# A Hymba block: FF2's forms staged by POOL four ahead, FF1's first products before the last transposes, the residual by adding transfers

## The chip, the cores and the metric

The kernel runs on one core of a Trainium2 chip. The metric is the device time of one execution in microseconds (us). TensorE (PE) multiplies, VectorE (DVE) and ScalarE (ACT) do arithmetic on tiles, GpSimd (POOL) and SyncE (SP) here mostly issue transfers (DMAs), each from its own queue and in its own order. TensorE's clock has two levels, 1.2 and 2.4 GHz; the profile gives the granted clock as a share of the full one.

## What is computed

One layer on x of 512 rows (SEQ) and 2048 columns (D), in float32:

```
u = rmsnorm(x, g1);  z = u @ w_in           # conv B, C, h, gla q, k, v, gate, decay
y = concat(conv_group(z), gla_group(z))
x = x + y @ w_out
h = rmsnorm(x, g2)
x = x + square(relu(h @ w_ff1)) @ w_ff2     # w_ff1: 2048 x 8192
out = rmsnorm(x, gf)
```

## The kernel before

**Products.** A float32 operand is split into a rounded part hi (ACT, a cast) and the rest lo (DVE, a subtraction); a product is hi x hi + hi x lo + lo x hi on PE. Both layers of the feed-forward part use a scheme of seven products in place of eight: an operand's four quarters are combined into seven *forms*, each product multiplies one form of the activations by one form of the weights, and sums of the results give the four quarters of the output. A product of a form is 24 matmuls of 128 x 128 by 128 x 256.

**The stages.** In-projection, gates, gated linear attention (`gla`), convolution; the out-projection in five chunks of columns (`out_chunk`, `token_major`), whose `put` adds the residual into xr (L602), squares it on ACT (L604) and stores it to x_keep. `h_pair(p)` transposes two 128-column tiles of xr on PE (htr, L563), scales them on DVE (h, L564), forms differences (L568 to L572) and splits the seven forms into Sh (ACT, L589) and Sl (DVE, L590). The last pair, 7, stands behind the whole out-projection.

FF1 runs over 32 groups g of two column tiles; a group loads four quarters of weights (SP, L494), forms sums (w_f, DVE, L509), splits them (hi_f L501, lo_f L502), and does seven products in the order 1, 5, 7, 3, 6, 2, 4 (`product`, L643, PE L653) into banks f1a to f1e. DVE and ACT combine, relu and square (L684 to L695). The seven forms of the result go to a_keep in HBM (POOL).

FF2 runs over four blocks (blk) of the contraction, in each over four column groups n and two halves grp: seven products each (`product2`, PE L747), the last half of block 3 with half the length. `form(blk, grp, f)` loads a form back from a_keep into st (SP, L729), casts ah (ACT, L735) and subtracts al (DVE, L736). Of the seven forms of a half every second is loaded into one of two stage buffers, the others into tiles of `act` that FF1's or an earlier block's forms held. `form` is called behind the product whose slots it takes over: the other half's forms during n = 0, the next block's during the last half of n = 3. `evict` (L768) sums the results into four tiles c, which POOL adds to c_keep in HBM (L774, L776); in block 3 tiles s are loaded from c_keep (L839), c is added into them by a transfer (L780), and `residual` (L756, DVE) adds s times r2 to x3, which was loaded from x_keep (L835). A last stage (PE e, L75 to L77) multiplies what is left of the contraction, adds, normalizes and writes.

**What sets the order.** The program is written in the order of the products; a scheduler then sets each engine's own order, and pools set which tile must be free. The weights' hi and lo have three buffers each, the raw quarters four, the sums w_f two. Lines that the change touches: L372 (GLA's states, pool of two), L603 (squares into a bank of tag "one"), L620 (`h_pair(7)`), L630 (PSUM pools change from `front` to `fb`), L644 to L656 (`product`), L718 to L738 (`form`), L751 to L758 (`residual`).

Of the kernel before, what the change touches and what calls it, by code (L numbers as in the profile page):

```python
# [8 lines left out]
F32 = mybir.dt.float32  # L9
# [5 lines left out]
P = 128  # L15
# [24 lines left out]
def hymba_kernel(  # L40
# [150 lines left out]
    with tc.tile_pool(name="mix", bufs=1) as mix:  # L191
# [167 lines left out]
        def gla(h):  # L359
# [4 lines left out]
            for c in range(NCHUNK):  # L364
                i = c // 2
                r = slice(c % 2 * CHUNK, (c % 2 + 1) * CHUNK)
                kv = bank(f"kv_{c}{h}", "one")
                T.matmul(
                    kv[:, :DV], kd[r, i, h * DK : (h + 1) * DK], vv[h // 2][r, i, cv],
                    start=True, stop=True,  # L370
                )
                st = mix.tile([P, DV], F32, name=f"st_{c}{h}", tag="st", bufs=2)  # L372
                if c == 0:
                    V.tensor_copy(st, kv[:, :DV])
                else:
# [221 lines left out]
    with tc.tile_pool(name="n2", bufs=1) as n2:  # L597

        def out_chunk(n, wsrc, w0, nunit, ncol, ktu, hook, ready=()):
            def put(i, b):  # L600
                xc = xs[n][i]
                V.tensor_tensor(out=xc, in0=b[:, :ncol], in1=xc, op=ALU.add)  # L602
                sq = bank(f"sq2_{n}{i}", "one")  # L603
                S.activation(sq[:, :ncol], xc, AF.Square, accum_out=ss2[:, i, n : n + 1])  # L604
                nc.gpsimd.dma_start(x_keep[i][:, chunks[n]], xc)

            token_major(yt, wsrc, w0, nunit, ncol, ktu, f"op{n}", put, hook, None, ready)
# [10 lines left out]
        first_forms = block_forms(w_ff1, 0, 1024, "f1_0")  # L618
        ready = {f: first_forms(f) for f in (1, 5, 7)}
        h_pair(7, n2)  # L620
        a2 = n2.tile([P, NT], F32, name="a2", tag="a2")
# [7 lines left out]
    late.close()  # L629
    front.close()  # L630
    fb = ctx.enter_context(tc.tile_pool(name="fb", bufs=1, space=PSUM, reuse_waits="tile"))

# [4 lines left out]


    with tc.tile_pool(name="f1", bufs=1, reuse_waits="tile") as f1:
        for g in range(NPAIR):  # L640
            forms = block_forms(w_ff1, 4 * g, 1024, f"f1_{g}") if g else first_forms

            def product(f, dst, start, pairs=range(8)):  # L643
                if g or f not in ready:  # L644
                    ready[f] = forms(f)
                hi, lo = ready[f]
                if 7 in pairs:
                    del ready[f]
                for p in pairs:
                    c = slice(p * P, (p + 1) * P)  # L650
                    sh, sl = hforms[p][f]
                    for m, (l, r) in enumerate(((hi, sh), (hi, sl), (lo, sh))):
                        T.matmul(  # L653
                            dst[:, :HALF], l[:, c], r, start=start and p == m == 0,
                            stop=p == 7 and m == 2, skip_group_check=True,
                        )  # L656
# [4 lines left out]
            ba, bc, bd, bb, be = (fbank(f"f1{k}_{g}") for k in "acdbe")  # L661
# [46 lines left out]


    PLACE = {1: 0, 2: 1, 4: 2, 7: 3, 5: 4, 6: 5, 3: 6}  # L710
    ORDERS = ((1, 3, 2, 5, 7, 6, 4), (1, 6, 5, 3, 7, 2, 4))
    first = [(hf, f"h{n}") for n in range(14)]
    second = [(act, f"s{k + 8 * m}") for e in range(2) for k in range(e, 8, 2) for m in range(2)]

    def in_slot(slot, name, dt=F32R):
        return slot[0].tile([P, 4, HALF], dt, name=name, tag=slot[1])

    with tc.tile_pool(name="ff", bufs=1, reuse_waits="tile") as ff:  # L718

        def form(blk, grp, f):  # L720

            n = ORDERS[grp].index(f)
            m = 2 if (blk, grp) == (3, 1) else 4
            name = f"st_{blk}{grp}{f}"
            if n % 2 and (blk, grp) != (3, 1):
                raw = in_slot(second[14 + n // 2 % 2], name, F32)
            else:
                raw = stage.tile([P, 4, HALF], F32, name=name, tag="st", bufs=2)
            nc.sync.dma_start(raw[:, :m, :], a_keep[2 * blk + grp][PLACE[f]][:, :m, :])  # L729
            if m == 2:  # L730
                t = in_slot(second[n], f"a{blk}{grp}{f}")
                hi, lo = t[:, 0:2, :], t[:, 2:4, :]
            else:
                hi, lo = (in_slot((first, second)[grp][2 * n + e], f"a{'hl'[e]}{blk}{grp}{f}") for e in range(2))
            S.copy(hi[:, :m, :], raw[:, :m, :])  # L735
            V.tensor_tensor(out=lo[:, :m, :], in0=raw[:, :m, :], in1=hi[:, :m, :].bitcast(F32), op=ALU.subtract)  # L736
            aforms[blk, grp, f] = hi, lo

# [62 lines left out]

        aforms = {}
        x3t = None
        for f in ORDERS[0]:
            form(0, 0, f)
        for blk in range(4):
            for n in range(4):
                dst = {f: fbank(f"f2_{blk}{n}{f}") for f in ORDERS[1]}
                had = {}
                for grp in range(2):  # L810
# [6 lines left out]
                    for f in ORDERS[grp]:  # L817
# [50 lines left out]
        for g in range(2):  # L868
            raw = stage.tile([P, 4, HALF], F32, name=f"st_e{g}", tag="st", bufs=2)
            nc.sync.dma_start(raw, a_last[g])  # L870
# [3 lines left out]
        for n in order[1:]:  # L874
            last_weights(n)
        gft = [stage.tile([P, 4, HALF], F32, name=f"gft{c}", tag="st", bufs=2) for c in range(2)]
        for c in range(2):
# [115 lines left out]
```

## Time and profile before

| | us |
|---|---|
| median of 3 runs (2109.1 to 2111.61) | 2111.08 |
| the profiled execution | 2109.2 |
| its span in the trace | 2107.5 |
| PE busy in it | 2070.4 |
| DVE busy | 1489.1 |
| ACT busy | 885.2 |
| POOL busy | 130.3 |

PE is busy for 98% of the span, so a step matters by what it does to PE's stops and to PE's clock. Three kinds of views are used: lists of waits (for whom an engine stood idle, how long in total, how often, the longest), windows (the busy time of each engine in a stretch, the mean granted clock, the busy share of the 16 DMA engines), and timelines (single instructions). In a timeline a row with x2 or x3 holds that many instructions, and the bracket gives the idle time ahead of it and what ended it.

### The profile page before, as it was taken

Reading aid. Unit: us, or ns where it says so; the run is one execution under the profiler, and the core shown is the slowest. Engines: PE = TensorE matmul, PEld = TensorE weight load, DVE = VectorE, ACT = ScalarE, POOL = GpSimd, SP = SyncE. Lnnn points to the kernel's source line nnn. Section 1 sums busy time; section 2 is a strip of 40 time slices with the busy share of each in tenths; the row PEclk is TensorE's granted clock in tenths of the full one; section 3 lists DMA queues with packets and bytes.
Section 4 is the critical chain, followed back from the end, with each engine's and each line's share of the span. In section 5 each row is a group of like instructions: output and inputs, shape, how many; then the busy total and the mean of one; then the engine's idle time right before and its main releaser. Section 6 shows DMA issues by size and latency. Waiting matters only on the chain. (4 is left out here: it accounts for less than half of the span.)

```text
span 2107.5 us, 34328 instructions
## 1 busy us (share of the span) xinstructions
PE 2070.4 (98%) x14408; PEld 1920.4 (91%) x14408; DVE 1489.1 (71%) x1740; ACT 885.2 (42%) x1106; POOL 130.3 (6%) x197
## 2 busy tenths in 40 slices
PE   8999999999999999999999999998999999999998
PEld 7988878778788899999999999998999999999996
DVE  5232226656664458888888888888789789888987
ACT  6242213212233334555555455555344345344343
POOL 0000000000010000000000000000000100103210
PEclk9999999999999999999999999999999999999999
DMA  7323222222253333544544544547456657667762
GB/s 296 90 80 100 90 86 85 80 80 89 72 159 122 121 117 114 180 153 145 164 153 137 165 152 143 163 156 255 144 166 216 148 158 219 166 158 237 182 187 101
DMA packets 90427, 307.11 MB, mean 146 GB/s; under 512 B 10773, under 2 KB 10821, under 8 KB 89760
## 3 DMA queue, kind: packets, MB, share of 16 engines
q1 hardware_dynamic: 69120, 242.64, 36.9%
q0 software_dynamic: 21152, 62.28, 10.5%
q8 instruction: 112, 1.84, 0.4%
q14 instruction: 43, 0.35, 0.1%
HBM read 252.19 MB, written 49.55 MB: 143 GB/s over the span
## 5 line engine op out<-in xcount | busy, mean ns | idle before, releaser
L747 PE MATMUL f<-hi_f,ah 128*128 128x256 f32 x1568 | 442.2, 282 | 10.9 <-ACT hi_f L501 5.6
L747 PE MATMUL f<-lo_f,ah 128*128 128x256 f32 x1568 | 444.0, 283 | 4.5 <-DVE lo_f L502 4.5
L747 PE MATMUL f<-hi_f,al 128*128 128x256 f32 x1568 | 441.1, 282 | 0.0
L502 DVE TENSOR_TENSOR lo_f<-w_f,hi_f 128x1024 fp32r<-128x1024 f32 (+1 forms) x256 | 304.2, 1191 | 144.3 <-ACT hi_f L501 142.8
L501 ACT CAST hi_f<-w_f 128x1024 fp32r<-128x1024 f32 (+1 forms) x256 | 261.8, 1024 | 337.0 <-PE f L747 113.9
L747 PEld LDWEIGHTS f<-hi_f,ah 128*128 128x128 f32 x1568 | 297.0, 189 | 12.9 <-ACT hi_f L501 7.2
L747 PEld LDWEIGHTS f<-lo_f,ah 128*128 128x128 f32 x1568 | 296.5, 189 | 6.9 <-DVE lo_f L502 6.5
L747 PEld LDWEIGHTS f<-hi_f,al 128*128 128x128 f32 x1568 | 297.1, 190 | 0.0
L501 ACT CAST hi_f<-raw_f 128x1024 fp32r<-128x1024 f32 (+1 forms) x192 | 196.6, 1025 | 197.5 <-PE f L747 84.3
L502 DVE TENSOR_TENSOR lo_f<-raw_f,hi_f 128x1024 fp32r<-128x1024 f32 (+1 forms) x192 | 227.9, 1187 | 25.9 <-ACT hi_f L501 25.9
L509 DVE TENSOR_TENSOR w_f<-raw_f,raw_f 128x1024 f32<-128x1024 f32 (+1 forms) x128 | 152.4, 1190 | 12.9 <-DMA raw_f<-in_w_ff 9.7
L509 DVE TENSOR_TENSOR w_f<-w_f,raw_f 128x1024 f32<-128x1024 f32 (+1 forms) x128 | 152.4, 1190 | 3.3
L653 PE MATMUL f1c<-Sh,hi_f 128*128 128x256 f32 x512 | 144.2, 282 | 0.9 <-ACT q L676 0.9
L653 PE MATMUL f1a<-Sh,hi_f 128*128 128x256 f32 x512 | 144.9, 283 | 0.0
L653 PE MATMUL f1a<-Sh,lo_f 128*128 128x256 f32 x512 | 144.9, 283 | 0.0
L653 PE MATMUL f1a<-Sl,hi_f 128*128 128x256 f32 x512 | 144.7, 283 | 0.0
L653 PE MATMUL f1c<-Sh,lo_f 128*128 128x256 f32 x512 | 144.2, 282 | 0.2 <-DVE lo_f L502 0.2
L653 PE MATMUL f1c<-Sl,hi_f 128*128 128x256 f32 x512 | 144.0, 281 | 0.0
L75 PE MATMUL tm_op<-hi_op,yh 128*128 128x512 f32 (+1 forms) x304 | 106.2, 349 | 0.0
L76 PE MATMUL tm_op<-lo_op,yh 128*128 128x512 f32 (+1 forms) x304 | 105.3, 346 | 0.0
L77 PE MATMUL tm_op<-hi_op,yl 128*128 128x512 f32 (+1 forms) x304 | 105.0, 345 | 0.0
L653 PEld LDWEIGHTS f1c<-Sh,hi_f 128*128 128x128 f32 x512 | 96.8, 189 | 1.1 <-ACT q L676 1.1
(360 smaller groups left out, 4857.8 us busy)
## 6 DMA issues: line engine op xcount, KB each, us to landing
raw_f<-in_w_ff SPq DMA_DIRECT2D x240, 512.0 KB, 3.6
a_keep<-y POOLq DMA_DIRECT2D x30, 896.0 KB, 5.1
st<-a_keep SPq DMA_DIRECT2D x49, 512.0 KB, 4.5
c_keep<-c POOLq DMA_DIRECT2D x48, 256.0 KB, 5.3
raw_op<-in_w_out SPq DMA_DIRECT2D x22, 512.0 KB, 3.6
raw_og<-in_w_feat SPq DMA_DIRECT2D x16, 512.0 KB, 3.6
raw_cc<-in_w_feat SPq DMA_DIRECT2D x16, 512.0 KB, 3.6
raw_ch<-in_w_feat SPq DMA_DIRECT2D x16, 512.0 KB, 3.7
```

Source lines behind the costliest of these rows:

```text
L75: T.matmul(dst, l[0], r[0], start=start, stop=False)
L76: T.matmul(dst, l[0], r[1], start=False, stop=False)
L77: T.matmul(dst, l[1], r[0], start=False, stop=stop)
L501: S.copy(hi[:, :n], src)
L502: V.tensor_tensor(out=lo[:, :n], in0=src, in1=hi[:, :n].bitcast(F32), op=ALU.subtract)
L509: V.tensor_tensor(out=w, in0=in0, in1=in1, op=ALU.add)
L653: T.matmul(dst[:, :HALF], l[:, c], r, start=start and p == m == 0, stop=p == 7 and m == 2, skip_group_check=True,)
L747: T.matmul(d, l[:, k, t], r[:, c], start=grp == k == i == e == 0, stop=grp == 1 and k == m - 1 and e == 2, skip_group_check=True,)
```

## The change

1. GLA's states get four buffers.
2. The squares of `put` go into the bank that held the sum, not into one of tag "one".
3. The products 1, 5 and 7 of FF1's group 0 over pairs 0 to 6 (63 matmuls) are written ahead of `h_pair(7)`. Group 0 uses banks of the `front` pools; these close at group 1.
4. Forms of FF2 are loaded by POOL into one of four stage buffers (`stage_form`); the load of form q + 4 is issued behind the split of form q (`split_form`), and an agenda says behind which product each form is split. The old `form` goes.
5. For n < 3 `residual` scales s by r2 on ACT and lets a transfer of POOL add it to x3.

```diff
-                st = mix.tile([P, DV], F32, name=f"st_{c}{h}", tag="st", bufs=2)
+                st = mix.tile([P, DV], F32, name=f"st_{c}{h}", tag="st", bufs=4)
...
-                sq = bank(f"sq2_{n}{i}", "one")
-                S.activation(sq[:, :ncol], xc, AF.Square, accum_out=ss2[:, i, n : n + 1])
+                S.activation(b[:, :ncol], xc, AF.Square, accum_out=ss2[:, i, n : n + 1])
...
         ready = {f: first_forms(f) for f in (1, 5, 7)}
+        def multiply(f, dst, start, pairs=range(8)):
+            hi, lo = ready[f]
...
+        first_banks = {1: bank("f1a_0", "one"), 5: bank("f1c_0", "one"), 7: bank("f1d_0")}
+        for f in (1, 5, 7):
+            multiply(f, first_banks[f], True, range(7))
         h_pair(7, n2)
...
-    front.close()
-    fb = ctx.enter_context(tc.tile_pool(name="fb", bufs=1, space=PSUM, reuse_waits="tile"))
...
+    sequence = [(blk, grp, f) for blk in range(4) for grp in range(2) for f in ORDERS[grp]]
+
+    def stage_form(q):
+
+        blk, grp, f = sequence[q]
+        m = 2 if (blk, grp) == (3, 1) else 4
+        raw = stage.tile([P, 4, HALF], F32, name=f"st_{blk}{grp}{f}", tag="st", bufs=4)
+        nc.gpsimd.dma_start(raw[:, :m, :], a_keep[2 * blk + grp][PLACE[f]][:, :m, :])
+        staged[q] = raw, m
+
+    def split_form(q):
+        blk, grp, f = sequence[q]
+        raw, m = staged.pop(q)
...
+        S.copy(hi[:, :m, :], raw[:, :m, :])
+        V.tensor_tensor(out=lo[:, :m, :], in0=raw[:, :m, :], in1=hi[:, :m, :].bitcast(F32), op=ALU.subtract)
+        aforms[blk, grp, f] = hi, lo
+        if q + 4 < len(sequence):
+            stage_form(q + 4)
...
+    agenda = {-10: [lambda: [stage_form(q) for q in range(4)]]}
+    for q in range(len(sequence)):
+        blk, k = divmod(q, 14)
+        if k >= 7:
+            at = 56 * blk + int((0 if blk else 2) + 1.4 * (k - 7))
+        else:
+            at = 56 * blk - 14 + int(5 + 1.35 * k) if blk else k - 4
+        agenda.setdefault(at, []).append(lambda q=q: split_form(q))
...
+            if g == 1:
+                front.close()
+                fb = ctx.enter_context(tc.tile_pool(name="fb", bufs=1, space=PSUM, reuse_waits="tile"))
...
             if g == 0:
-                for f, b in ((1, ba), (5, bc), (7, bd)):
-                    product(f, b, True, range(7))
...
+                if n < 3:
+                    S.activation(c[:, i, :], c[:, i, :], AF.Copy, scale=r2[:, k : k + 1])
+                    nc.gpsimd.dma_start(xc, c[:, i, :], accum_op=ALU.add)
+                    continue
...
-                        if (n, grp) == (0, 0):
-                            form(blk, 1, f)
-                        if (n, grp) == (3, 1) and blk < 3:
-                            form(blk + 1, 0, ORDERS[0][ORDERS[1].index(f)])
+                        keep_agenda(7 * (8 * blk + 2 * n + grp) + ORDERS[grp].index(f))
```

The agenda and the scheduler move instructions at three places. The first is PE's order at the end of the out-projection (tm_op43 is the last of its banks, xr_40 to xr_43 are the last sums, htr the transposes, f1a, f1c, f1d the banks of products 1, 5, 7; Sh1 and Sh70 are high parts of pairs 0 to 3 and of pair 7). Before:

```order
L77 MATMUL tm_op43_5330<-hi_op4_3_5566,yl_7_4078 128x256
L563 MATMUL htr_14_5660<-ident_72,xr_40_4160 128x128
...
L563 MATMUL htr_15_5666<-ident_72,xr_40_4160 128x128
...
L563 MATMUL htr_14_5660<-ident_72,xr_43_4163 128x128
L563 MATMUL htr_15_5666<-ident_72,xr_43_4163 128x128
L653 MATMUL f1a_0_5707<-Sh1_4547,hi_f1_01_5643 128x256
L653 MATMUL f1a_0_5707<-Sl1_4548,hi_f1_01_5643 128x256
L653 MATMUL f1a_0_5707<-Sh1_4547,lo_f1_01_5644 128x256
```

and now:

```order
L77 MATMUL tm_op43_5314<-hi_op4_3_5550,yl_7_4078 128x256
L628 MATMUL f1a_0_5639<-Sh1_4543,hi_f1_01_5623 128x256
L628 MATMUL f1a_0_5639<-Sl1_4544,hi_f1_01_5623 128x256
L628 MATMUL f1a_0_5639<-Sh1_4543,lo_f1_01_5624 128x256
...
L628 MATMUL f1d_0_5641<-Sh60_5541,hi_f1_07_5635 128x256
L628 MATMUL f1d_0_5641<-Sl60_5542,hi_f1_07_5635 128x256
L628 MATMUL f1d_0_5641<-Sh60_5541,lo_f1_07_5636 128x256
L563 MATMUL htr_14_5706<-ident_72,xr_40_4160 128x128
...
L563 MATMUL htr_14_5706<-ident_72,xr_43_4163 128x128
...
L563 MATMUL htr_15_5712<-ident_72,xr_43_4163 128x128
L628 MATMUL f1c_0_5640<-Sh70_5721,hi_f1_05_5629 128x256
L628 MATMUL f1a_0_5639<-Sh70_5721,hi_f1_01_5623 128x256
L628 MATMUL f1d_0_5641<-Sh70_5721,hi_f1_07_5635 128x256
L628 MATMUL f1c_0_5640<-Sl70_5722,hi_f1_05_5629 128x256
```

The eight transposes stood ahead of all 72 matmuls of the first three products; now 63 of these stand ahead of them, and behind them the nine that need pair 7.

The second is ACT's order from the last group of FF1 into FF2 (ah_blk,grp,form are casts of forms; hi_f1_31x are weights of FF1's last group, hi_f2_000x those of FF2's first products). Before:

```order
L735 CAST ah002_13215<-st_002_13213 128x1024
...
L735 CAST ah007_13227<-st_007_13225 128x1024
L501 CAST hi_f2_0001_13258<-raw_f2_0000_13250 128x1024
...
L735 CAST ah004_13239<-st_004_13237 128x1024
L735 CAST ah011_13288<-st_011_13286 128x1024
...
L735 CAST ah003_13209<-st_003_13207 128x1024
L735 CAST ah005_13221<-st_005_13219 128x1024
L735 CAST ah015_13392<-st_015_13390 128x1024
L735 CAST ah017_13428<-st_017_13426 128x1024
L501 CAST hi_f2_0007_13398<-w_f2_0007_13396 128x1024
```

and now:

```order
L683 CAST ah001_13087<-st_001_12876 128x1024
...
L683 CAST ah003_13122<-st_003_12878 128x1024
...
L683 CAST ah002_13162<-st_002_12880 128x1024
...
L683 CAST ah005_13197<-st_005_12882 128x1024
L501 CAST hi_f1_314_13169<-w_f1_315_12997 128x1024
L683 CAST ah007_13256<-st_007_13091 128x1024
L501 CAST hi_f2_0001_13228<-raw_f2_0000_13220 128x1024
L683 CAST ah006_13290<-st_006_13126 128x1024
```

The form 003, which the second product of FF2 needs, was cast behind 002, 007, 004 and 011; now it is the second, ahead of three weights of FF1's last group.

The third is ACT's order in block 3 where n goes from 0 to 1 (s_0q are the sums of n = 0, hi_f2_310x the weights of n = 1). Before:

```order
L501 CAST hi_f2_3103_19339<-raw_f2_3102_19305 128x1024
L501 CAST hi_f2_3102_19369<-raw_f2_3103_19307 128x1024
L501 CAST hi_f2_3105_19401<-w_f2_3105_19399 128x1024
L501 CAST hi_f2_3107_19433<-w_f2_3107_19431 128x1024
L501 CAST hi_f2_3106_19462<-w_f2_3105_19399 128x1024
```

and now:

```order
L501 CAST hi_f2_3103_19321<-raw_f2_3102_19285 128x1024
L792 ACTIVATE s_00_19113<-s_00_19113,r2_4185 128x256 x2
L501 CAST hi_f2_3102_19353<-raw_f2_3103_19287 128x1024
L792 ACTIVATE s_02_19117<-s_02_19117,r2_4185 128x256 x2
L792 ACTIVATE s_01_19115<-s_01_19115,r2_4185 128x256 x2
L501 CAST hi_f2_3105_19387<-w_f2_3105_19385 128x1024
L792 ACTIVATE s_03_19119<-s_03_19119,r2_4185 128x256 x2
L501 CAST hi_f2_3107_19421<-w_f2_3107_19419 128x1024
L501 CAST hi_f2_3106_19450<-w_f2_3105_19385 128x1024
```

The pairs that scale s stand between the casts of weights; those of s_03 are ahead of the cast for product 7. On POOL, the issues of the same stretch were four and are now:

```order
L819 DMA s_02_19117<-c2_30_19232 128x512
L819 DMA s_01_19115<-c1_30_19251 128x512
L793 DMA x3_00_19097<-s_00_19113 128x256
L793 DMA x3_10_19099<-s_00_19113 128x256
L793 DMA x3_20_19101<-s_02_19117 128x256
L819 DMA s_03_19119<-c3_30_19271 128x512
L793 DMA x3_30_19103<-s_02_19117 128x256
L793 DMA x3_01_19098<-s_01_19115 128x256
L793 DMA x3_11_19100<-s_01_19115 128x256
```

The transfer that adds c3 to s_03 stands behind three that add s to x3, and so behind ACT's pairs for s_00 and s_02.

## Rows read from the trace of the kernel before

**Rows 1.** The page, busy us (share) x instructions of each engine.
```profile
PE 2070.4 (98%) x14408; PEld 1920.4 (91%) x14408; DVE 1489.1 (71%) x1740; ACT 885.2 (42%) x1106; POOL 130.3 (6%) x197
```

**Rows 2.** Waits of PE, whole span: us in total, times, longest.
```profile
PE f L747 <- ACT hi_f L501: 5.6, 8, 0.9
PE f L747 <- DVE lo_f L502: 5.6, 11, 0.9
```

**Rows 3.** Windows: us, busy PE, PEld, DVE, ACT, POOL, clock, DMA share, GB/s.
```profile
780.00:800.00 20.00, 16.51 (x125) 16.00 (x124) 17.57 (x33) 8.26 (x17) 2.17 (x4) 0.91 0.08 27
1430.00:1450.00 20.00, 15.38 (x118) 15.18 (x117) 16.22 (x16) 14.17 (x16) 0.55 (x1) 0.91 0.90 314
1600.00:1620.00 20.00, 17.73 (x139) 16.58 (x139) 18.81 (x18) 7.43 (x8) 0.54 (x1) 1.00 0.77 250
1760.00:1780.00 20.00, 17.92 (x148) 17.28 (x146) 17.90 (x17) 8.61 (x10) 1.08 (x2) 1.00 0.92 254
1930.00:1940.00 10.00, 8.24 (x54) 7.83 (x54) 6.56 (x8) 4.71 (x6) 6.03 (x12) 0.83 0.97 306
```

**Rows 4.** Timeline of PE, 784 to 802: start us, duration us, instruction.
```profile
785.09 0.28 PE L77 MATMUL tm_op<-hi_op,yl 128*128 128x256 f32 x1
...
789.81 0.44 PE L563 MATMUL htr<-ident,xr 128*128 128x128 f32 x2 [3.15 <-DVE xr L602]
...
794.10 0.28 PE L653 MATMUL f1c<-Sh,hi_f 128*128 128x256 f32 x1
794.22 0.29 PE L653 MATMUL f1c<-Sl,hi_f 128*128 128x256 f32 x1
...
801.18 0.39 PE L653 MATMUL f1c<-Sh,hi_f 128*128 128x256 f32 x1 [0.85 <-ACT q L676]
```

**Rows 5.** Timeline of DVE, 779 to 803.
```profile
787.33 2.09 DVE L590 TENSOR_TENSOR Sl<-h,Sh 128x768 fp32r<-128x768 f32 x2
...
790.80 1.40 DVE L564 SCALAR_TENSOR_TENSOR h<-htr,g2t,r1b 128x512 f32<-128x512 f32 x2
...
792.20 1.22 DVE L509 TENSOR_TENSOR w_f<-raw_f,raw_f 128x1024 f32<-128x1024 f32 x1
...
796.34 1.22 DVE L590 TENSOR_TENSOR Sl<-h,Sh 128x1024 fp32r<-128x1024 f32 x1
```

**Rows 6.** Timeline of ACT, 779 to 803.
```profile
789.85 0.39 ACT L604 ACTIVATE sq<-xr 128x256 f32<-128x256 f32 x1 [0.95 <-DVE xr L602]
...
799.54 1.05 ACT L501 CAST hi_f<-raw_f 128x1024 fp32r<-128x1024 f32 x1 [3.23 <-PE f1c L653]
```

**Rows 7.** Timelines of PE and DVE at the change from FF1 to FF2.
```profile
1439.00 0.58 PE L747 MATMUL f<-hi_f,ah 128*128 128x256 f32 x1 [4.62 <-ACT ah L735]
...
1426.46 0.42 DVE L684 TENSOR_TENSOR u<-f1b,q 128x256 f32<-128x256 f32 x1
...
1453.83 1.22 DVE L502 TENSOR_TENSOR lo_f<-w_f,hi_f 128x1024 fp32r<-128x1024 f32 x1
```

**Rows 8.** Waits of ACT in 1885 to 1945 (block 2 to 3).
```profile
ACT a L735 <- DMA st<-a_keep: 15.0, 7, 4.1
```

**Rows 9.** DMA: issues (KB, median us to landing); landings of tile s, of c_keep.
```profile
st<-a_keep SPq DMA_DIRECT2D x49, 512.0 KB, 4.5
...
gft<-in_gf POOLq DMA_DIRECT2D x2, 512.0 KB, 4.1
...
DMA to landing us min/median/max: 2.9/3.9/5.7
...
DMA to landing us min/median/max: 2.3/4.9/8.5
```

**Rows 10.** Timelines of POOL and PE in block 3, n = 0 to 1.
```profile
1988.24 1.76 POOL L780 DMA_DIRECT2D s<-c  x2 [0.30 <-DVE c L768]
...
1988.64 0.38 PE L747 MATMUL f<-hi_f,ah 128*128 128x256 f32 x1 [0.90 <-ACT hi_f L501]
...
1993.35 0.34 PE L747 MATMUL f<-lo_f,ah 128*128 128x256 f32 x1
```

More of the change, by code (lines that the diff above doesn't have):

```diff
@@ L619, in hymba_kernel @@
         ready = {f: first_forms(f) for f in (1, 5, 7)}
+        def multiply(f, dst, start, pairs=range(8)):
+            hi, lo = ready[f]
+            if 7 in pairs:
+                del ready[f]
+            for p in pairs:
+                c = slice(p * P, (p + 1) * P)
+                sh, sl = hforms[p][f]
+                for m, (l, r) in enumerate(((hi, sh), (hi, sl), (lo, sh))):
+                    T.matmul(
+                        dst[:, :HALF], l[:, c], r, start=start and p == m == 0,
+                        stop=p == 7 and m == 2, skip_group_check=True,
+                    )
+        first_banks = {1: bank("f1a_0", "one"), 5: bank("f1c_0", "one"), 7: bank("f1d_0")}
+        for f in (1, 5, 7):
+            multiply(f, first_banks[f], True, range(7))
         h_pair(7, n2)
@@ L636, in hymba_kernel, with in_slot @@
     stage = ctx.enter_context(tc.tile_pool(name="stage", bufs=1, reuse_waits="tile"))
+    PLACE = {1: 0, 2: 1, 4: 2, 7: 3, 5: 4, 6: 5, 3: 6}
+    ORDERS = ((1, 3, 2, 5, 7, 6, 4), (1, 6, 5, 3, 7, 2, 4))
+    first = [(hf, f"h{n}") for n in range(14)]
+    second = [(act, f"s{k + 8 * m}") for e in range(2) for k in range(e, 8, 2) for m in range(2)]
+    def in_slot(slot, name, dt=F32R):
+        return slot[0].tile([P, 4, HALF], dt, name=name, tag=slot[1])
+    aforms = {}
+    staged = {}
+    sequence = [(blk, grp, f) for blk in range(4) for grp in range(2) for f in ORDERS[grp]]
@@ new lines, in stage_form @@
+    def stage_form(q):
[7 more added lines that the diff above has]
+        raw, m = staged.pop(q)
+        n = ORDERS[grp].index(f)
+        if m == 2:
+            t = in_slot(second[n], f"a{blk}{grp}{f}")
+            hi, lo = t[:, 0:2, :], t[:, 2:4, :]
+        else:
+            hi, lo = (in_slot((first, second)[grp][2 * n + e], f"a{'hl'[e]}{blk}{grp}{f}") for e in range(2))
+        S.copy(hi[:, :m, :], raw[:, :m, :])
[3 more added lines that the diff above has]
+            stage_form(q + 4)
@@ L639, in hymba_kernel, with keep_agenda @@
+    agenda = {-10: [lambda: [stage_form(q) for q in range(4)]]}
[3 more added lines that the diff above has]
+            at = 56 * blk + int((0 if blk else 2) + 1.4 * (k - 7))
+        else:
+            at = 56 * blk - 14 + int(5 + 1.35 * k) if blk else k - 4
+        agenda.setdefault(at, []).append(lambda q=q: split_form(q))
+    def keep_agenda(at):
+        for task in agenda.pop(at, ()):
+            task()
     with tc.tile_pool(name="f1", bufs=1, reuse_waits="tile") as f1:
@@ L640, in hymba_kernel @@
         for g in range(NPAIR):
+            if g == 1:
+                front.close()
+                fb = ctx.enter_context(tc.tile_pool(name="fb", bufs=1, space=PSUM, reuse_waits="tile"))
             forms = block_forms(w_ff1, 4 * g, 1024, f"f1_{g}") if g else first_forms
             def product(f, dst, start, pairs=range(8)):
-                if g or f not in ready:
+                if f not in ready:
                     ready[f] = forms(f)
-                hi, lo = ready[f]
+                multiply(f, dst, start, pairs)
@@ L647, in product @@
                 if 7 in pairs:
[L648 to L656, printed above, removed]
+                    keep_agenda(7 * (g - NPAIR) + FORMS.index(f))
@@ L658, in half @@
             def half(name, bufs=2):
                 return f1.tile([P, HALF], F32, name=f"{name}_{g}", tag=name, bufs=bufs)
-            ba, bc, bd, bb, be = (fbank(f"f1{k}_{g}") for k in "acdbe")
+            if g == 0:
+                ba, bc, bd = (first_banks[f] for f in (1, 5, 7))
+                bb, be = (bank(f"f1{k}_0") for k in "be")
+            else:
+                ba, bc, bd, bb, be = (fbank(f"f1{k}_{g}") for k in "acdbe")
             y = f1.tile([P, 8, HALF], F32, name=f"y_{g}", tag="y", bufs=2)
@@ L706, in hymba_kernel @@
             )
[L710 to L716, printed above, removed]
-    with tc.tile_pool(name="ff", bufs=1, reuse_waits="tile") as ff:
[L720 to L737, printed above, removed]
+    with tc.tile_pool(name="ff", bufs=1, reuse_waits="tile") as ff:
         def product2(blk, grp, f, m, dst, hi, lo):
@@ L800, in evict @@
                 block(3, p, had["v"], ALU.subtract)
-        aforms = {}
         x3t = None
-        for f in ORDERS[0]:
-            form(0, 0, f)
         for blk in range(4):
@@ L868, in hymba_kernel @@
         for g in range(2):
-            raw = stage.tile([P, 4, HALF], F32, name=f"st_e{g}", tag="st", bufs=2)
+            raw = stage.tile([P, 4, HALF], F32, name=f"st_e{g}", tag="st", bufs=4)
             nc.sync.dma_start(raw, a_last[g])
@@ L875, in hymba_kernel @@
             last_weights(n)
-        gft = [stage.tile([P, 4, HALF], F32, name=f"gft{c}", tag="st", bufs=2) for c in range(2)]
+        gft = [stage.tile([P, 4, HALF], F32, name=f"gft{c}", tag="st", bufs=4) for c in range(2)]
         for c in range(2):
```

## The prediction

> **What bounds the kernel now.** I read the page's busy times first: TensorE (PE) works 2070.4 of 2107.5 us [rows 1], so all that a change of order can win is the 37.1 us in which PE stands, and what PE loses while its clock is low. Next, the waits of PE: apart from one wait at the program's start, which the change does not touch, the largest are for the weight parts hi_f and lo_f (5.6 us each, in small pieces) [rows 2], and there is one long wait each for an activation part ah and for a transposed chunk, taken up in B and A. Then the windows show where they lie: at the last transposes (780 to 800), at the change from FF1 to FF2 (1430 to 1450), and at the three changes of block in FF2 [rows 3]. There the reader is to see two things: PE's busy time against the width, and the granted clock. Where the mean clock is 0.91 over 20 us, part of the stretch ran at 1.2 instead of 2.4 GHz, and the work lost is 0.09 x 20 = 1.8 us; at 1930 to 1940 it is 0.17 x 10 = 1.7 us. At the two block changes where PE lost about 2 us in smaller pieces the clock stayed at 1.00. So a long stop here costs itself and about 1.7 us more, the small ones only themselves.
>
> A product of a form is 24 matmuls. At full clock they start 0.12 us apart (794.10 and 794.22 in [rows 4]), so a product takes 2.83 us.
>
> **Parts that cost nothing.** Four buffers for GLA's states: no wait of PE names that place, so 0. Squares written into their own bank: the bank's next user comes a whole chunk later, 0; it is what makes room for part A.
>
> **A, the last transposes.** Before, PE ended the out-projection at 785.09 plus one matmul, waited 3.15 us for the last sum xr, and started FF1's first product at 790.0 at the low clock [rows 4]. Now 63 matmuls (7.5 us) stand between. They start at 785.2; 25 of them need nothing late and end at 788.2; the next needs the low part of pair 6, which VectorE (DVE) finishes at 787.33 + 2.09 = 789.4 [rows 5]: a stop of 1.3. The other 38 end at 793.9, the eight transposes at 794.8. So the 3.15 us wait is filled, but the chain behind the transposes now has nothing beside it. Before, from the first h operation (790.80) to the last low part (796.34 + 1.22) it took 6.76 us, in which a weight sum of 1.2 us and nine tiny operations stood [rows 5]; in the new order those are ahead of it. Without them it is some 5 us, so the last low part is there at 800.0 instead of 797.6. Behind it the sequence is as before: product 1 must end before ScalarE (ACT) may cast hi_03 into its buffer, which before began at 799.54 [rows 6], and product 3 needs that and the copy q5. It went on at 801.18 [rows 4]; with low parts 2.4 us later and nine matmuls (1.1 us) now run in an order that frees hi_03's buffer sooner, it will at about 802.55: +1.4. The new stop of some 5 us is longer than the one that cost the clock before, and lies after it; the old low-clock stretch is already in the 801.2, so I add one more: +1.7. **A: +3.0**; bounds 0 (no low clock, the chain 1.4 shorter) and +5 (every operation of the chain with a wait on the other engine).
>
> **B, FF1 to FF2.** PE waits 4.62 us for ah of the form 003 at 1439.0 [rows 7], and then runs at the low clock. Its load could only start when a slot came free at FF1's end. In the new order 003 is split second, during FF1's last group. The ideal is 4.6 + 1.7 = 6.3 us. But DVE must still do the same work: from u at 1426.46 to the end of lo_0004 (1453.83 + 1.22) are 28.6 us [rows 7], of which 3.8 are idle in 1430 to 1450 [rows 3]; packed tight it ends at 1451.3, 3.7 us sooner. PE without stops asks for lo_0004 six products after FF1's end, 1431.5 + 17.0 = 1448.5. So PE now waits for DVE instead of for one late load: the gain is 3.7 at best plus what the low clock gave back, less the waits of DVE on ACT's casts. **B: -3.0**; bounds -1 and -6.3.
>
> **C, the three block changes.** ACT waits there for the loads of forms, at the third one 15.0 us in 7 waits [rows 8], and DVE, PE follow. The casts and subtractions stand at nearly the same places in ACT's and DVE's order as before, so what changes is that a load is issued four forms ahead, in one of four buffers. PE's idle time was 2.3 us at 1600 to 1620, 2.1 at 1760 to 1780, 1.8 at 1930 to 1940, there with 1.7 of clock [rows 3]. If the loads are early all of it goes: -2.3 - 2.1 - 3.5 = -7.9; the bounds are that and 0. I take not the whole: at the first change DVE is busy 18.8 of 20 us, so the load can't be all of the cause; 1.0 us of that stop I leave. **C: -6.9.** A form costs POOL one issue; it stands behind an eviction's adding transfer, which waits for DVE, by one product (2.83 us) at most, of a lead of four.
>
> A load of 512 KB took 4.5 us from SP's queue and 4.1 from POOL's [rows 9], so the queue as such costs nothing. The Trainium skill ("SBUF — State Buffer", the trap "DVE blocks DMA") speaks against the change: a transfer issued from POOL gets no descriptors while DVE runs an operation in a 2-port mode, and it advises SP or ACT. By that rule, if every form waited for one DVE operation of 1.2 us, B would gain 1.2 less and the sum be -5.2; the two POOL loads gft show no such delay, but DVE was not full beside them.
>
> **D, the residual.** For n = 0 to 2, 24 DVE operations become 24 ACT operations, in pairs, and 24 adding transfers on POOL. DVE's share was not what stopped PE at n's changes: PE's first matmul there goes ahead of its weights by its own order, which the change leaves. On ACT the pair for s_03 stands ahead of the cast hi_3107, and ACT waits for s_03's adding transfer. The previous s transfers went out at 1988.24, 0.88 us each [rows 10]; behind them POOL issues x_00, x_10, x_20, and so s_03 at about 1994.2. It lands in 3.9 us by the median of s [rows 9]: 1998.1; the pair 0.8 (two of 0.39 [rows 6]), the cast 1.05, the subtraction 1.15: lo_3107 at 2001.1. PE begins 3103 at 1993.35 [rows 10] and after 71 matmuls of 0.118 asks for it at 2001.8. The slack is 0.7 us, so the median costs nothing and a landing near the longest of s (5.7) costs 1.1 per change. **D: +1.0**; bounds 0 and +4.
>
> **E.** At the ends of products where PE's order alternated between two banks it now runs straight. What is left of PE's waits for weights when B, C and the three changes of n (0.90 each [rows 10]) are taken off [rows 2] is 11.2 - 6.2 - 2.7 = 2.3 us: **-0.5**, bounds +1 and -1.5.
>
> **Sum.** 3.0 - 3.0 - 6.9 + 1.0 - 0.5 = -6.4 us. The profiled execution took 2109.2 us (its span of 2107.5 and 1.7 around it), so 2102.8; it lay 1.9 under the median of the three runs, so for a median I say 2111.08 - 6.4 = **2104.7 us**.
>
> **Rivals.**
> 1. *The chain at A is shorter and DVE at B is not the limit*: A 0, B -6.3, C -7.9, the rest as above: -13.7, 2097.4 us. For it: DVE has 3.8 idle us at B. Against: the chain at A has no cover whatever. Chance 0.12.
> 2. *The transfers are the bound at the block changes, not when they are issued.* The DMA engines are 0.77, 0.92 and 0.97 busy there [rows 3]; a load four ahead moves other loads back, and PE then waits for weights. C and B shrink to -3 together, A stays: +0.5, 2111.6 us, no change. It is also the case in which the change does not do what it says: in ACT's and DVE's order the splits of blocks 1 to 3 hardly moved, so the "longer stretch" is one only at B. The Trainium skill ("Trainium Kernel Development and Optimization", Key Constraints) says the same in general: queues of SP, ACT and POOL share 16 DMA engines, and a second queue saves issue time only; the busy shares of those windows agree with it. Against: ACT's waits for forms are named [rows 8], and the change moves no byte more for them. Chance 0.20.
> 3. *Slower: the adding transfers land late, and ACT stands behind them.* Beside the other traffic of the blocks, adding transfers took up to 8.5 us (c_keep [rows 9]). At 8.5 instead of 3.9 lo_3107 is 3.9 us late at each of three changes of n, and stops of that length cost 1.7 of clock as well: 3 x 5.6 = 16.8 in place of 1.0, so -6.4 - 1.0 + 16.8 = +9.4, 2120.5 us. Without the clock's part the sum changes sign at a landing of about 7 us (3 x 2.5 us late); up to 4.6 it costs nothing. For it: 24 more transfers with a read each in that stretch. Against: s's longest was 5.7. Chance 0.12.
>
> **Numbers.** My forecast has 0.56, and its own range is 2099 to 2109. What a measurement of this kernel tells from no change is about 0.2%, 4.2 us, so faster means under 2106.9. Of the forecast's chance 0.05 lies above that: faster 0.51 + 0.12 = 0.63, same 0.05 + 0.20 = 0.25, slower 0.12. The whole range goes from rival 1 into the part of rival 3 with fewer late changes: 2096 to 2114; some 0.05 lies below and 0.11 above.
>
> **What would show it.** A: one stop of 4 to 6 us at about 795 to 800 in place of those at 786 and 789, and a low clock after it. B: no wait for ah; at most 3 us for lo_f at about 1448 to 1452. C: no wait of ACT for forms of over 1 us, PE over 19 of 20 us at the block changes, clock 1.00 at 1930. D: a wait of ACT for s ahead of the fifth cast, with PE going on. I am wrong if PE's stops at the block changes stay while ACT's waits for forms are gone (DVE or the transfers were the cause), if FF1's first products don't fill the wait at 785, or if PE stands over 2 us at changes of n.

## The result, and the profile after

The changed kernel takes 2116.84 us (median of 10 runs, 2112.49 to 2118.74), the kernel before 2110.45 us in the same comparison: a ratio of 1.0033, 95% interval 1.0024 to 1.0041. It is slower by 6.4 us, where 6.4 us less was forecast, and outside the range. The profiled execution of the changed kernel took 2113.75 us, 3.1 below its median, against 2109.2 before; the spans differ by 4.5 us. The traces can account for these 4.5; the other 2 us of the medians' difference no trace shows.

The page's busy times of the changed kernel, and then its list of PE's waits:

```profile
PE 2071.2 (98%) x14408; PEld 1921.2 (91%) x14408; DVE 1481.9 (70%) x1716; ACT 894.1 (42%) x1130; POOL 181.2 (9%) x277
```

```profile
PE f L782 <- DVE lo_f L502: 11.0, 13, 1.4
PE f L782 <- ACT hi_f L501: 6.8, 7, 3.0
...
PE f1c L628 <- ACT Sh L589: 4.1, 1, 4.1
```

Against [rows 1], PE's busy time is the same, POOL has 51 us more and DVE 7 less. The wait for ah of [rows 7] is gone (none stands in the list), but against [rows 2] the waits for weights rose from 5.6 + 5.6 to 11.0 + 6.8 us. So a wait for activations became waits for weights.

Where this happens is seen from a fixed point of each stage: a copy q on ACT, which stands in every group of FF1 and every n of FF2. I take the start of each in both traces; the change is behind (+) or ahead (-) by, in us: FF1's second group +3.0 and all of FF1 so; FF2 block 0, n = 0 +1.2, n = 1 +0.7; block 1, n = 0 -0.2; block 2, n = 0 +0.6; block 3, n = 0 **-4.4**, n = 1 **+0.8**, n = 2 +1.8, n = 3 +2.4; the last stage's start +4.1, the end +4.5. The copies of block 3, n = 0 and n = 1, first before, then in the changed kernel:

```profile
1948.99 0.59 ACT L787 COPY q<-f 128x512 f32<-128x512 f32 x1 [0.73 <-PE f L747]
1980.46 0.59 ACT L787 COPY q<-f 128x512 f32<-128x512 f32 x1 [0.74 <-PE f L747]
```

```profile
1944.60 0.59 ACT L826 COPY q<-f 128x512 f32<-128x512 f32 x1 [0.73 <-PE f L782]
1981.22 0.59 ACT L826 COPY q<-f 128x512 f32<-128x512 f32 x1 [0.74 <-PE f L782]
```

The windows of the changed kernel (columns as in [rows 3]):

```profile
780.00:800.00 20.00, 15.02 (x118) 14.07 (x116) 18.02 (x33) 7.51 (x16) 2.16 (x4) 0.92 0.08 27
800.00:805.00 5.00, 4.17 (x16) 3.66 (x17) 2.94 (x4) 3.48 (x5) 0.00 (x0) 0.50 0.18 34
1430.00:1450.00 20.00, 19.11 (x162) 18.91 (x161) 19.24 (x21) 15.36 (x18) 6.90 (x13) 1.00 0.89 307
1600.00:1620.00 20.00, 17.78 (x146) 17.17 (x145) 19.10 (x18) 8.04 (x8) 3.22 (x6) 1.00 0.73 235
1760.00:1780.00 20.00, 17.62 (x145) 17.01 (x144) 17.52 (x16) 7.61 (x8) 3.17 (x6) 1.00 0.81 223
1930.00:1940.00 10.00, 10.00 (x87) 10.00 (x86) 8.34 (x9) 2.76 (x4) 6.23 (x12) 1.00 1.01 333
1950.00:1960.00 10.00, 5.58 (x31) 5.09 (x31) 6.86 (x9) 3.38 (x5) 3.73 (x5) 0.70 0.71 190
```

The long stops at FF1's end and at 1930 are gone (PE 19.11 of 20 and 10.00 of 10 us, clock 1.00, against 15.38 and 8.24). The two block changes between stand as they were (17.78 and 17.62 against 17.73 and 17.92). The low-clock stretch by the last transposes lies later than before and is longer: the clock is 0.50 over the whole of 800 to 805, where it was 1.00. A new one lies at 1950 to 1960, where PE stood 4.4 of 10 us and the clock was 0.70, against 1.00 before. The one at the start of FF2 has not gone but moved, to 1450 to 1460 (0.83).

The timelines show the stop behind the last transposes and the one at 1950 to 1960, and what ended them, PE first, then DVE and POOL at the second:

```profile
798.91 0.58 PE L628 MATMUL f1c<-Sh,hi_f 128*128 128x256 f32 x1 [4.06 <-ACT Sh L589]
...
802.48 0.58 PE L628 MATMUL f1c<-Sh,hi_f 128*128 128x256 f32 x1 [0.66 <-ACT q L739]
...
1954.92 0.58 PE L782 MATMUL f<-hi_f,ah 128*128 128x256 f32 x1 [3.05 <-ACT hi_f L501]
...
1952.60 1.23 DVE L509 TENSOR_TENSOR w_f<-raw_f,raw_f 128x1024 f32<-128x1024 f32 x1 [3.77 <-DMA raw_f<-in_w_ff]
...
1942.51 1.07 POOL L911 DMA_DIRECT2D gft<-in_gf  x2
```

Before the first, 63 matmuls and the transposes are done, and nothing covers the chain h, Sh, Sl. Before the second, DVE stood 3.77 us for the weights of block 3, n = 1, in front of everything else in its order. Ten microseconds earlier POOL had issued the last stage's two loads gft, 512 KB each. Before the change they went out at 2034 and 2038 us, because they had to wait for one of only two stage buffers. With four buffers nothing holds them back. The prediction did not see that move. That the loads of the weights were late because of gft is tested next.

### The profile page after: what moved, and what is told of

It is laid out like the page before. It is cut to its first block, busy times and chain, and to the rows that moved or that the text cites. A ratio compares the mean times of both kernels' runs of the same rounds, so it can differ in the third digit from the quotient of the medians.

```text
span 2112.0 us, 34355 instructions
## 1 busy us (share of the span) xinstructions
PE 2071.2 (98%) x14408; PEld 1921.2 (91%) x14408; DVE 1481.9 (70%) x1716; ACT 894.1 (42%) x1130; POOL 181.2 (9%) x277
## 4 chain that ended last, share of the span: by engine, by line
PE 82%; DVE 6%; issue 4%; DMA 4%; ACT 2%; POOL 1%; ACTq 0%; POOLq 0%; DVEq 0%
PE f L782 15%; PE f1c L628 8%; PE f1a L628 8%; PE f1d L628 4%; PE f1e L628 4%; PE f1b L628 4%; PE tm_op L75 3%; PE tm_op L76 3%; PE tm_op L77 3%; DVE lo_f L502 2%; PE fm_ch L75 2%; PE fm_cc L75 2%; DVE al L684 2%; DVE w_f L509 2%; PE tm_v L76 1%
```

## The experiments

All ratios are to runs of the kernel before on the same chip, so that different comparisons can be set beside each other; the changed kernel's is 1.0033. One thousandth is 2.1 us.

**1. The early loads.** One-column copies make gft wait for the splits of the last stage:

```diff
         for c in range(2):
+            V.tensor_copy(gft[c][:, 0, 0:1], a[2 * c + 1][1][1][:, 0:1].bitcast(F32))
             nc.gpsimd.dma_start(
```

> Edit: the changed kernel with the two loads gft (512 KB each) made to wait, by a one-column copy, for the last stage's activation splits, as they did before the change; with four stage buffers they had moved from about 2034 to 1942 us. Theory T1 (transfers bound the way into block 3): the 1 MB of gft stood ahead of the weights of n = 1, which DVE waited 3.8 us for; without it the stops of PE of 3.05 and 1.37 us at 1951 to 1957 and their low clock go, 3 to 5 us less than the changed kernel. Rival T2 (DVE's order bounds: the sum w_f stands ahead of the subtractions whatever the transfers do): the stop stays, within 1 us of the changed kernel.

Measured: ratio 1.0009, interval 1.0000 to 1.0018, 5 us less. gft goes out at 2039 and 2044, and DVE's wait and PE's stops shrink (the clock of 1950 to 1960 is 0.91 instead of 0.70):

```profile
1953.50 1.23 DVE L509 TENSOR_TENSOR w_f<-raw_f,raw_f 128x1024 f32<-128x1024 f32 x1 [0.91 <-DMA raw_f<-in_w_ff]
...
1956.53 0.38 PE L782 MATMUL f<-hi_f,ah 128*128 128x256 f32 x1 [0.90 <-ACT hi_f L501]
1957.77 0.38 PE L782 MATMUL f<-lo_f,a 128*128 128x256 f32 x1 [0.86 <-DVE lo_f L502]
```

T1 holds, though in part of the stops only. In its own trace this kernel lost as much at another place, the start of FF2: a stop of 2.72 us at 1454, where the changed kernel's trace has 0.45 (the clock is low behind both, 0.82 and 0.83 over 1450 to 1460). Nothing was edited there, and PE's and ACT's orders are the same; with one trace of each kernel, that this stop differs from run to run is the likely reading, not a shown one.

**2. The first products.** The loop over `multiply` is moved behind the r2 operations; the separate banks stay:

```diff
-        for f in (1, 5, 7):
-            multiply(f, first_banks[f], True, range(7))
         h_pair(7, n2)
...
         V.tensor_tensor(out=r2, in0=r2, in1=r2, op=ALU.mult)
+        for f in (1, 5, 7):
+            multiply(f, first_banks[f], True, range(7))
```

> Edit: the changed kernel with the 63 first products written behind the last transposes again, but in their own banks, so that the scheduler may put 22 of them between the transposes of the first six and of the last two tiles. Theory (the uncovered chain behind the transposes costs): the stop of 4.06 us at 794.6 shrinks to about 1 us, no low clock behind it, FF1's second group starts 4 to 6 us sooner than in the changed kernel, and the time is less by as much. Rival: what PE gains there is given back at the change to FF2, where DVE is the bound: less by 1 us or nothing.

Measured: 1.0011, interval 1.0002 to 1.0020, 4.6 us less. FF1's second group comes 3.1 us sooner than in the changed kernel (4 to 6 were expected), as early as before the change.

```profile
785.37 1.18 PE L563 MATMUL htr<-ident,xr 128*128 128x128 f32 x6
789.36 0.39 PE L628 MATMUL f1a<-Sl,hi_f 128*128 128x256 f32 x1 [0.56 <-DVE Sl L590]
789.82 0.38 PE L563 MATMUL htr<-ident,xr 128*128 128x128 f32 x2
796.23 0.38 PE L628 MATMUL f1c<-Sh,hi_f 128*128 128x256 f32 x1 [1.15 <-ACT Sh L589]
```

The scheduler put 22 matmuls into the wait ahead of the last transposes, and kept 41 for the chain behind them: the stop ahead of Sh is 1.15 instead of 4.06 us. A low clock comes even so, but later and for less long (0.57 over 800 to 804, 1.00 after it). The rival is not ruled out: in the traces the lead over the changed kernel is 3.7 us at block 0, 1.5 at block 1 and 0.1 at the end. The 4.6 us go by the medians; the profiled execution of this kernel lay 1.7 us above its own, the changed kernel's 3.1 below.

**3. The residual.** DVE's 24 operations return:

```diff
-                if n < 3:
-                    S.activation(c[:, i, :], c[:, i, :], AF.Copy, scale=r2[:, k : k + 1])
-                    nc.gpsimd.dma_start(xc, c[:, i, :], accum_op=ALU.add)
-                    continue
```

> Edit: the changed kernel with the residual's 24 additions on DVE again instead of scalings on ACT and adding transfers on POOL. Theory (the adding transfers hold up ACT's casts and fill the queues in block 3): PE's additional stops at 2002.5 and 2041 and the later weights of the last stage go, 2 to 3.5 us less than the changed kernel. Rival (DVE, 24 operations of 0.4 us fuller, is what bounds block 3): within 1 us, or more by 1.

Measured: 1.0011, interval 1.0002 to 1.0020, 4.6 us less, more than the 2 to 3.5 of the theory. From the copy q of block 3, n = 1, to the start of the last stage the changed kernel loses 3.4 us against before; this one gains 0.3. PE's waits from 1985 to 2066, of the changed kernel and of this one:

```profile
PE f L782 <- DVE lo_f L502: 2.8, 5, 1.0
PE f L782 <- ACT hi_f L501: 1.8, 2, 0.9
PE e L75 <- ACT w10h L884: 0.6, 1, 0.6
PE e L76 <- DVE w01l L885: 0.4, 1, 0.4
PE e L76 <- DVE w20l L885: 0.3, 1, 0.3
```

```profile
PE f L782 <- ACT hi_f L501: 2.0, 2, 1.1
PE f L782 <- DVE lo_f L502: 1.0, 4, 0.4
PE e L75 <- ACT w10h L880: 0.5, 1, 0.5
```

**4. Transfers or ACT's order?** ACT scales, DVE adds:

```diff
-                    nc.gpsimd.dma_start(xc, c[:, i, :], accum_op=ALU.add)
+                    V.tensor_tensor(out=xc, in0=c[:, i, :], in1=xc, op=ALU.add)
                     continue
```

> Edit: the changed kernel with ACT still scaling s for n < 3, but DVE adding it to x3 (24 additions) instead of 24 adding transfers. It tells what of the residual's cost is the transfers and what is ACT waiting for s ahead of casts. Theory T3 (the transfers: x is read and written by them beside the weights' loads, and s comes free later, so the next c_keep loads and the last weights are late): 3 to 5 us less than the changed kernel, as with the residual on DVE. Rival T4 (ACT's order): within 1.5 us of the changed kernel.

Measured: 1.0020, interval 1.0009 to 1.0031, between the two and not clear of either. Its trace speaks for the transfers in the stretch where they lie: from block 3, n = 1, to the last stage it loses 0.25 us, about as DVE's residual (-0.3), and not 3.4. But ACT's waits for s, in 1944 to 2060, also fell, from 19.7 to 11.8 us, so the two causes are not wholly apart. By the times the difference of 2.7 us to the changed kernel is just below what T3 wanted.

**5. What is left.** The edits of 1, 2 and 3 together, with no other; the forms are still staged by POOL.

> Edit: all three together: of the change only the forms staged by POOL four ahead and the separate banks are left, with gft late. If the three terms are separate and add up, some 9 to 13 us less than the changed kernel, 3 to 6 us less than the kernel before. Rival (the gain at the change from block 2 to 3 is given back whatever is done, by the transfers): not below the kernel before by more than 2 us.

Measured: 0.9983, interval 0.9975 to 0.9992; 10.5 us less than the change, 3.6 less than before. The three terms do not add up (5 + 4.6 + 4.6 = 14.2), but most of it does.

**6. POOL's queue.** One word: the load in `stage_form` is issued by SP instead of POOL, once in 5 and once in the full change.

```diff
-        nc.gpsimd.dma_start(raw[:, :m, :], a_keep[2 * blk + grp][PLACE[f]][:, :m, :])
+        nc.sync.dma_start(raw[:, :m, :], a_keep[2 * blk + grp][PLACE[f]][:, :m, :])
```

> Edit: staging_only with the forms' loads issued from SP's queue instead of POOL's; four buffers and four ahead as before. If POOL's queue costs (descriptors held up while DVE works, or loads behind evictions' transfers): 2 us or more less than staging_only. If POOL's queue is what helps (a load does not wait behind weight loads, nor they behind it): 2 us or more above staging_only. If the four buffers are all that matters: within 1.5 us.

> Edit: the changed kernel as it is, with the forms' loads issued from SP's queue; gft early, residual by transfers, first products early as in the change. Theory (POOL's queue is a cost of its own: 7 us between staging_only and forms_on_sp): 4 to 8 us less than the changed kernel, near the kernel before. Rival (in the full change the queue is hidden behind the other costs): within 2 us of the changed kernel.

Measured: 0.9955 (0.9942 to 0.9967), 5.9 us less than the same with POOL; and in the full change 0.9998 (0.9989 to 1.0007), 7.4 us less than the change. PE's and DVE's orders are the same in 5 and 6, and ACT's but for one cast of a form that changes places with one of a weight. At the change from block 1 to 2, PE's waits in 1740 to 1800, first with POOL, then with SP:

```profile
PE f L782 <- DVE lo_f L502: 3.2, 3, 1.5
PE f L782 <- ACT hi_f L501: 0.4, 1, 0.4
```

```profile
PE f L782 <- DVE lo_f L502: 0.9, 1, 0.9
PE f L782 <- ACT hi_f L501: 0.5, 1, 0.5
```

The same rows of the changed kernel, and of the changed kernel with SP:

```profile
PE f L782 <- DVE lo_f L502: 3.2, 3, 1.4
PE f L782 <- ACT hi_f L501: 0.5, 1, 0.5
```

```profile
PE f L782 <- DVE lo_f L502: 1.1, 2, 0.9
PE f L782 <- ACT hi_f L501: 0.4, 1, 0.4
```

By the copies q the full change with SP gains 1.9, 1.6 and 4.7 us on the kernel before at the three block changes; with POOL it was 0.8, -0.7 and 5.0.

Behind the stops of 5 stands the cast of a form that landed late; in each of the two timelines the first row is its load's issue, the second ACT's cast (the second of SP's two issues, at 1756.4, is the next form's):

```profile
1753.14 0.54 POOL L671 DMA_DIRECT2D st<-a_keep  x1 [1.61 <-ACT hi_f L501]
...
1760.40 1.05 ACT L683 CAST ah<-st 128x1024 fp32r<-128x1024 f32 x1 [3.72 <-DMA st<-a_keep]
```

```profile
1751.20 5.52 SPq L671 DMA_DIRECT2D st<-a_keep  x2
...
1756.03 1.05 ACT L683 CAST ah<-st 128x1024 fp32r<-128x1024 f32 x1 [2.47 <-DMA st<-a_keep]
```

A load goes out when its buffer comes free, and its split frees the buffer of the load four on: the buffers form a ring, whose lap is issue, landing, cast and subtraction, and a delay of a load is handed on to the load four later. That is worked out from the order, not shown by a run of its own. From a buffer's last reader to the issue it is 0.3 to 0.55 us for most loads on POOL and 0.03 on SP. To land took 7.2 us for this form on POOL, where the evictions' adding transfers were issued ahead of and behind it, and 4.8 on SP; over all forms of full size the medians are alike (4.8 and 4.8 us). How much of the 6 us is the issue and how much the shared queue, or what the evictions' transfers gain when POOL's queue is theirs alone, no run separates.

**7. The lead.** Experiment 5 with two stage buffers (for every user of the tag) and a lead of two.

```diff
-        if q + 4 < len(sequence):
-            stage_form(q + 4)
+        if q + 2 < len(sequence):
+            stage_form(q + 2)
```

> Edit: staging_only with two stage buffers and each load issued two forms ahead. If the lead of four is what took ACT's waits at the change from block 2 to 3 away: the stop at 1931 comes back in part, 2 to 4 us more than staging_only, and at the change from FF1 to FF2 another 1 to 3. If any issue off SP's queue does: within 1.5 us.

Measured: 1.0038 (1.0026 to 1.0051), 11.6 us more than with four. The buffers and the lead are worth that much on POOL's queue, more than expected, and at all three block changes. From FF1 to FF2 it is the other way than expected: by block 0, n = 1, the kernel with two is 2.8 us ahead of 5 in the traces. So four early loads cost something there.

**8. DVE at the block changes.** In experiment 5, half of the low part of each form of blocks 1 to 3 (but for the short last half) is left out, and ACT fills its place with a copy; the result is another.

```diff
+        d = 2 if blk and m == 4 else m
-        V.tensor_tensor(out=lo[:, :m, :], in0=raw[:, :m, :], in1=hi[:, :m, :].bitcast(F32), op=ALU.subtract)
+        V.tensor_tensor(out=lo[:, :d, :], in0=raw[:, :d, :], in1=hi[:, :d, :].bitcast(F32), op=ALU.subtract)
+        if d < m:
+            S.copy(lo[:, d:, :], raw[:, d:, :])
```

> Edit: staging_only; in blocks 1 to 3 DVE subtracts the low part of only half of each form, the other half is filled by a copy on ACT (so half of the low parts hold the activations themselves, and the result is another). DVE has 7.5 us less work at each change of block, the transfers are the same. Theory T5 (DVE bounds the changes from block 0 to 1 and 1 to 2): PE's stops there (2.2 and 3.6 us) shrink below 1 us each, 4 to 5 us less than staging_only. Rival T1 (transfers bound there too): within 1.5 us.

Measured: 0.9928 (0.9915 to 0.9942), 11.6 us less than experiment 5. PE has not one wait in 1560 to 1630 and 1740 to 1800. So DVE's work sets these two stops on POOL's queue, and the bytes moved, the same as in 5, do not. It does not follow that when a load is issued is of no account: in 6 the same stops shrink with DVE's work unchanged, and a shorter split frees its buffer sooner, so both edits shorten the lap of the ring. In the traces the two changes take 8 us less, 3 and 5; that is nearly twice what was expected from the stops alone, and why is not shown. The whole traces differ by only 5.2 us: the profiled execution here was the slowest of its five, that of 5 the fastest of its eleven.

**9. Taking work off DVE.** In 6, POOL subtracts the last three forms of the second half of blocks 1 and 2:

```diff
-        V.tensor_tensor(out=lo[:, :m, :], in0=raw[:, :m, :], in1=hi[:, :m, :].bitcast(F32), op=ALU.subtract)
+        E = G if blk and grp and n >= 4 and m == 4 else V
+        E.tensor_tensor(out=lo[:, :m, :], in0=raw[:, :m, :], in1=hi[:, :m, :].bitcast(F32), op=ALU.subtract)
```

> Edit: forms_on_sp, with the low parts of the last three forms of a block's second half (blocks 1 and 2) subtracted by POOL instead of DVE: 3.4 us less on DVE at two block changes. If DVE's work bounds these changes (stops left in forms_on_sp: 1.3 us at each): 1 to 2.5 us less than forms_on_sp. If POOL's operation is slow or holds DVE up: the same or 1 to 3 us more.

Measured: 0.9995 (0.9986 to 1.0004), 8.4 us more than 6. POOL's row and DVE's beside it:

```profile
1592.42 3.21 POOL L685 TENSOR_TENSOR al<-st,ah 128x1024 fp32r<-128x1024 f32 x1 [2.81 <-PE f L783]
...
1593.89 2.82 DVE L502 TENSOR_TENSOR lo_f<-raw_f,hi_f 128x1024 fp32r<-128x1024 f32 x1
1596.64 3.56 DVE L685 TENSOR_TENSOR al<-st,ah 128x1024 fp32r<-128x1024 f32 x1
```

DVE's operation of 1.21 us takes up to 3.56 beside POOL's.

**10. The agenda's stretch.** 1.9 products between splits instead of 1.4, in 6.

```diff
-            at = 56 * blk + int((0 if blk else 2) + 1.4 * (k - 7))
+            at = 56 * blk + int(1.9 * (k - 7) if blk else 2 + 1.4 * (k - 7))
...
-            at = 56 * blk - 14 + int(5 + 1.35 * k) if blk else k - 4
+            at = 56 * blk - 14 + int(1.5 + 1.9 * k) if blk else k - 4
```

> Edit: forms_on_sp, with the agenda stretched (1.9 instead of 1.4 products between splits). PE's order stays, on DVE some ten rows move by one to three places, since the splits already stand where slots come free. Theory: within 1 us of forms_on_sp. Rival (the stretch is what matters): the stops left at the block changes go, 2 us less.

Measured: 0.9968 (0.9957 to 0.9980), 2.7 us more than 6, which neither theory expected; the two intervals overlap. In its trace the stops at the first two block changes are about as in 6, and two new ones of 0.36 and 0.88 us stand at 1922 to 1926. A longer stretch shows no gain here.

**11. The first products in two parts,** in 6: product 1 and two pairs of 5 ahead of the last transposes, the rest behind.

```diff
-        for f in (1, 5, 7):
-            multiply(f, first_banks[f], True, range(7))
+        multiply(1, first_banks[1], True, range(7))
+        multiply(5, first_banks[5], True, range(2))
         h_pair(7, n2)
...
+        multiply(5, first_banks[5], False, range(2, 7))
+        multiply(7, first_banks[7], True, range(7))
```

> Edit: forms_on_sp, with product 1 and a part of product 5 written ahead of the last transposes and the rest behind them, all eight transposes together. Theory (what counts is that something covers the chain behind the transposes, not what fills the wait ahead): within 1 us of forms_on_sp, which has 22 matmuls between the transposes by the scheduler's choice. Rival: 1 to 2 us less, since the first six transposes' wait goes too.

Measured: 2098.72 us, 0.9951 (0.9938 to 0.9963), the same as 6 (2099.21) within the intervals. Both beat the two kernels: 10 us less than before, some 17 less than the change.

## Why the prediction was wrong

By the copies q the 4.5 us between the two traces divide so: A +3.0, B -2.3, the three block changes -5.1 together, the first change of n in block 3 +5.2, and from there to the end +3.8. The forecast had +3.0, -3.0, -6.9, nothing, and +0.5 for D and E.

- **A, +3.0: right in size and cause.** Product 3 went on at 802.48 (forecast 802.55), with the low clock behind it; FF1 ran 3.0 us late to its end. Experiment 2 undoes it.
- **B, -3.0: right in the main.** The lag shrinks by 2.3 us from FF1 to block 0, n = 1; no wait for ah is left, and PE waits for lo_f from 1449 on, as said. It also waits for hi_f (0.45 and 0.56 us), and the clock is low at 1450 to 1460; that DVE alone is the bound there no run shows.
- **C, -6.9: 5.1 came, almost all at one place.** At block 2 to 3 the gain was 5.0 us (forecast 3.5), at the other two 0.8 and -0.7 (forecast 1.3 and 2.1). ACT's waits for loads fell at the first change from 9.1 to 5.1 us, and PE's stops stayed. That is half of the sign the prediction named for "DVE or the transfers were the cause". With SP's queue alone put back the gains are 1.9, 1.6 and 4.7 us (experiment 6), 8.3 together: so four buffers and four ahead are worth what C said and a little more, and what failed at the first two changes is the next point. DVE has a part, for which C left only 1.0 us where DVE stood 18.8 of 20 us busy: with half of its subtractions left out the stops go too (experiment 8).
- **The failing step: "the queue as such costs nothing".** This was enough by itself to make the difference. It was read from the medians of landings [rows 9], of 49 loads of forms on SP against two loads gft on POOL outside the blocks; the medians of the forms stayed alike on both queues. But a form's delay counts from the free buffer, and the ring hands it on (worked out in experiment 6, not shown apart). Undoing this one word brings the full change back to 0.9998, 7.4 us less. The sentence on one product of delay had the right place (behind an eviction's transfer) and called it covered by the lead of four.
- **The Trainium skill's rule** ("SBUF — State Buffer", the trap "DVE blocks DMA") warned of this queue, and its advice, SP's or ACT's queue, was right for SP's by 6 to 7 us; the price of one operation that the prediction put on it was too small. That descriptors were held up by DVE no row shows: the landings' medians do not differ.
- **D, +1.0: wrong in size and reason.** The slack of 0.7 us ahead of hi_3107 was the wrong place to look. The 24 adding transfers go with a loss of 3.4 us through the later weights of n = 2, n = 3 and the last stage; without the transfers, but with ACT still scaling and waiting for s, 0.25 is left (experiment 4). Rival 3 had the sign, the part and a price that was too high (16.8 us), with the wrong mechanism: no stop of 3.9 us at the changes of n.
- **Not in the sum at all: gft.** I counted the buffers' number for forms and not for the other users of the same tag. Two loads moved 92 us ahead into a stretch full of transfers (the DMA engines were 1.01 busy at 1930 to 1940) and took back the gain of C there (-4.4 to +0.8 us in one n; experiment 1). The kernel's text shows the cause: gft's tiles have the tag "st", and their line too went from two buffers to four. This is a piece of rival 2: behind the change from block 2 to 3 the transfers are the bound.
- **E, -0.5: wrong.** The last stage begins 1.7 us later against n = 3, with the weights late; these 1.7 us are a part of D's 3.4.
- **The two parts put at nothing** cost nothing that a trace shows: PE's last matmul of the out-projection starts at 784.82 us (785.09 before). No run undoes them alone.

By experiments the four costs are 7.4 (queue), 5 (gft), 4.6 (first products) and 4.6 us (adding transfers); together they are less than their sum, some 17 us, and the four stage buffers with the separate banks gain 10 us when these are gone. The forecast had 3.0 for the first products, 1.0 for the adding transfers and nothing for the other two.

## What to carry to other kernels

When a pool of buffers grows, list every tile that uses its tag: whatever waited for a buffer will move too, and a load that comes early is paid by the loads that are due. Price a ring of buffers by its lap, from the last reader of a buffer to the next use, and not by the median of the landing alone. Work moved ahead to fill one wait may uncover the chain that it used to cover: split it between both.

## What was not expected of the hardware

- A subtraction of 128x1024 took POOL 2.4 to 3.2 us and stretched DVE's of 1.21 us to as much as 3.56 us beside it.
- POOL issued most loads 0.3 to 0.55 us after their buffer was free, SP 0.03 us.
- The stop at the start of FF2 differs between two kernels that are the same there (the changed one and experiment 1): 0.45 us in one trace, 2.72 in the other. The changed kernel's ten runs spread over 6.3 us, those of the two best kernels, five each, over 3.4 and 2.3 us.
